# Bias row copies in 12 pieces behind the first attention's swaps, compression weights queued later, and idle products at the start

## The chip, the cores and the metric

One core of one Trainium2 chip runs the whole program once. The metric is the device time in microseconds of that core, as a median of several runs. TensorE (PE) multiplies matrices, VectorE (DVE), ScalarE (ACT) and GpSimd (POOL) do the elementwise work, and SyncE (SP) issues every data transfer of this kernel. A number such as L510 is a line of the kernel.

## The reference, cut to what matters

512 tokens of width 1024 go through a first block and then twice through a hybrid layer. All numbers are 32-bit floats.

```
# first block
h = rms_norm(x, pre_mix_g);  proj = h @ w_in          # q, k, v of two attentions, gates
oa = diff_attention(rope(qa), rope(ka), va)           # 4 heads of 128, causal
ob = softmax-weighted sum of three dilated windows over rope(qb), rope(kb), vb   # 3 groups x 4 heads
x = x + rms_norm((g_a * (oa @ w_a_out) + g_b * (ob @ w_b_out)) @ w_mix_out, post_mix_g)
u = causal_depthwise_conv(rms_norm(x, pre_ffn_g) @ w_up)
x = x + rms_norm((gelu(gate) * val) @ w_down, post_ffn_g)

# hybrid layer, twice
kc, vc = silu(blocks(k_cmp) @ cmp_w1) @ cmp_w2, ...   # the compression
logits = q @ k.T * scale + rel_bias[head, t5_bucket(distance)]   # windows of 512 and of 128
x = x + rms_norm((attentions * silu(z)) @ w_out, g_post)
```

The rotation `rope` pairs each row of a head with a partner row, so the kernel needs a copy of q and k with its rows swapped. The relative bias depends on the distance alone.

## The kernel before, in words

**Products.** Every large product keeps 32-bit precision by splitting both operands in a high and a low part: `mm3` issues three matmuls (L195 to L197) of 128 x 128 by 128 x 512. A weight tile of 512 KB is loaded into `wraw` (L169, three buffers), ScalarE rounds it to `whi` (L162), VectorE subtracts to `wlo` (L163), four buffers each. `fm` makes one tile of 128 output rows for all 512 tokens: 24 matmuls.

**Order.** The program is written stage by stage, and a planner orders each engine's instructions at compile time by a simulated timeline. So a load whose buffer is free can stand far ahead of its stage in the program. Within an engine, and on SP's queue, instructions then run strictly in that order; SP hands all its transfers to one hardware queue. `tc.issue_after(ins)` orders the instructions traced under it behind `ins` on the same engine.

**Start.** `ident` (L150), two halves of the first token tile (`load_x`, L357), the gain row `grow` (L366), first weights, more token tiles. Two products with a row of ones spread the gains (`g_pre`, L371). `pre_norm` makes each token tile's mean square, scales it (`xn`, L236), transposes it with `ident` on PE (`tp`, L224) and splits it to `hT`. The products `pv` for the values of the first attention follow.

**First attention** (L525 to L597). For each of four heads `a_project` makes q and k, each through `rope`: ScalarE copies the product to `rq` (L506), SP copies the swapped rows into `rs` (L510; four transfers here, two in the second attention), VectorE multiplies both with cosine and sine and adds (L512 to L521). `a_attend` of a head stands one head behind: scores (L544), subtract the maximum (L548), exponential, values. Products for the values of the second attention (`tm_cols(VB, ...)`) stand after head 0's projection.

**Bias and mask** (L599 to L602, written behind the first attention). `m_b` is the second attention's mask. `bias_tables` loads the buckets (`rb`, `hot`), makes the bias of each distance with three small products (`bv`, L398) and stores them to `vrow` in DRAM (L404). `bias_rows` writes each row 128 times to `spill` in DRAM (L409), in two DRAM to DRAM transfers of [4, 128, 640] and [8, 128, 384]. The hybrid layers read `spill` once, at L786, with a step that shifts each row.

**Second attention** (L607 to L687): `b_project` with six swaps for each head, `b_attend` with scores (L641, L645), the maximum (`nm`, L650), exponential and values.

**Later.** The gates and `w_mix_out`; the feed-forward loop over `w_up` (L748 to L757); `w_down` in `post_norm`; then the layers. There the compression reads its weights into four buffers `w1` of the tag `e4`, 16 transfers for each layer (L990); the first attention's outputs `oa` use the same tag before.

Of the kernel before, what the change touches and what calls it, by code (L numbers as in the profile page):

```python
# [9 lines left out]
F32 = mybir.dt.float32  # L10
# [84 lines left out]
def emit(tc, A, out):  # L95
    nc = tc.nc
# [13 lines left out]
    def c2(name, dt=F32):  # L110
        return bp.tile([128, 512], dt, name=name, tag="c2", bufs=16)
# [25 lines left out]
    def bank(tag, name):  # L137
        if tag == extra["tag"]:
            extra[tag] += 1
            if extra[tag] % 3 == 0:  # L140
                tag = "x"
        return pp.tile([128, 512], F32, name=name, tag=tag,
                       bufs={"pj": 2, "s": 2, "t": 2, "x": 1, "o": 1}[tag])
# [3 lines left out]


    ident = cp.tile([128, 128], F32, name="ident")
    nc.sync.dma_start(ident, A["c_ident"])  # L150
    mhalf = cp.tile([128, 4], F32, name="mhalf")
    nc.vector.memset(mhalf, -0.5)

# [2 lines left out]

    ahead = []
    evacuated = {}

    def split(src, hi, lo, engine=nc.vector):  # L160

# [3 lines left out]
    def wtile(src3):  # L165

        a, b = src3.shape[1], src3.shape[2]
        raw = wp.tile([128, a, b], F32, name="wraw", tag="wraw", bufs=3)
        nc.sync.dma_start(raw, src3)  # L169
        return raw  # L170

    def wsplit(raw):
# [95 lines left out]
    def gain(pool, name, src, off=0):  # L268
        g = pool.tile([128, D], F32, name=name, tag="gain", bufs=caps[pool].get("gain", 2))
        nc.sync.dma_start(g, bcast(src, D, off))  # L270
        return [g[:, u:u + 512] for u in (0, 512)]
# [77 lines left out]
    mp_stack, mp = phase("mp", r=4, pb=2, pt=4, qk=11, tb=5, P=2)  # L349
# [4 lines left out]
    def load_x(t):  # L354
        xt = [c2("xt") for _ in range(2)]
        for u in range(2):
            nc.sync.dma_start(xt[u], A["x"][0, t * 128:(t + 1) * 128, u * 512:u * 512 + 512])  # L357
        return xt

    def v_weights(c0, k0):  # L360
        return wtile(wrows(W1, PW, 0, k0, 2, c0, 512))


    xt = [load_x(0)]
    grow = mp.tile([1, D + 128], F32, name="grow", tag="P", bufs=caps[mp]["P"])
    nc.sync.dma_start(grow[:, 0:D], bass.AP(tensor=A["pre_mix_g"].tensor, offset=A["pre_mix_g"].offset,  # L366
                                    ap=[[D, 1], [1, D]]))
# [2 lines left out]
    for u in range(2):  # L370
        nc.tensor.matmul(g_pre[u], grow[:, D:], grow[:, u * 512:u * 512 + 512],  # L371
                         start=True, stop=True)
# [9 lines left out]
    spill = [dp.tile([4, 128, 640], F32, name="spill0"), dp.tile([8, 128, 384], F32, name="spill1")]  # L382
    vrow = [dp.tile([4, 640], F32, name="vrow0"), dp.tile([8, 384], F32, name="vrow1")]

    def bias_tables():
        rb = small("rb", 12, 1, mp)
        nc.vector.memset(rb, 1.0)
        rel = A["rel_bias_2"]
        nc.sync.dma_start(rb[0:32].rearrange("p (a b) -> p a b", b=1),
                          bass.AP(tensor=rel.tensor, offset=rel.offset,  # L390
                                  ap=[[1, 32], [32, 12], [1, 1]]))
        hot = [t2(mp, "pb", "hot") for _ in range(2)]
        wv = [os("wv") for _ in range(2)]
        for i in range(2):
            nc.sync.dma_start(hot[i][0:33], A["c_hot"][:, 512 * i:512 * i + 512])
        for i, c0, w, r0, m in ((0, 0, 512, 0, 4), (1, 0, 128, 0, 4), (1, 128, 384, 4, 8)):
            ps = bank("t", "bv")
            nc.tensor.matmul(ps[0:m, :w], rb[0:33, r0:r0 + m], hot[i][0:33, c0:c0 + w],  # L398
                             start=True, stop=True)
            nc.vector.tensor_copy(wv[i][0:m, c0:c0 + w], ps[0:m, :w])  # L400
        for dest, src in ((vrow[0][:, 0:512], wv[0][0:4]),
                          (vrow[0][:, 512:640], wv[1][0:4, 0:128]),
                          (vrow[1], wv[1][0:8, 128:512])):
            nc.sync.dma_start(dest, src)  # L404

    def bias_rows():

        for dest, src in zip(spill, vrow):
            nc.sync.dma_start(dest, src[:, None].to_broadcast(dest.shape))  # L409

    def hact(k):
        return hT[0][:, k], hT[1][:, k]
# [1 line left out]
    def tm_cols(c0, dest, dil=1):  # L414

        ws = {}
        for half in range(2):
            ps = [bank("pj", "pv") for _ in range(2)]  # L420
            for k0 in range(0, 8, 2):
                if not half:
                    ws[k0] = wsplit(c0 == VA and early.pop(k0, None) or v_weights(c0, k0))
                hi, lo = ws[k0]
                for e in range(2):
                    t = 2 * half + e
                    tok = slice(t * 128, (t + 1) * 128) if dil == 1 else slice(t, 512, 4)
                    for k in range(2):
                        mm3(ps[e], hT[0][:, k0 + k, tok], hT[1][:, k0 + k, tok],
                            hi[:, k], lo[:, k], k0 + k == 0, k0 + k == 7)  # L430
            for e in range(2):
                nc.scalar.copy(dest[2 * half + e], ps[e])
# [66 lines left out]
    nc.sync.dma_start(gdh, cols(A["diff_head_g"], 0, 1).rearrange("p a b -> p (a b)"))  # L499
    nc.vector.tensor_scalar(gdh, gdh, 1.0 - (0.8 - 0.6 * math.exp(-0.3 * 0)), None, op0=OP.mult)  # L500

    def rope(ps, cos, sin, sw, perm=None):


        q = t2(mp, "r", "rq")
        nc.scalar.copy(q, ps)  # L506
        s = t2(mp, "r", "rs")
        for b in range(0, 128, sw):
            o = b ^ sw
            nc.sync.dma_start(s[b:b + sw], q[o:o + sw])  # L510
        o = t2(mp, "qk", "qk")
        nc.vector.tensor_mul(q, q, cos)  # L512
        nc.vector.tensor_mul(s, s, sin)
        if perm is None:
            nc.vector.tensor_add(o, q, s)
        elif perm == "q":
            v = lambda a: a.rearrange("p (n i r) -> p n r i", n=4, r=4)
            nc.vector.tensor_add(o.rearrange("p (n r i) -> p n r i", n=4, r=4), v(q), v(s))
        else:
            v = lambda a: a.rearrange("p (j r) -> p r j", r=4)  # L520
            nc.vector.tensor_add(o.rearrange("p (r j) -> p r j", r=4), v(q), v(s))  # L521
        return o
# [64 lines left out]
        nc.scalar.activation(oa[h], pt, AF.Copy, scale=gdh)  # L587

    vb = [[c2("vb") for _ in range(4)] for _ in range(3)]
    prev = None  # L590
    for h in range(5):
        cur = a_project(h) if h < 4 else None
        if h == 0:
            tm_cols(VB, vb[0])
        if prev is not None:
            a_attend(h - 1, *prev)
        prev = cur  # L597

    m_b = mp.tile([128, 1536], F32, name="m_b")  # L599
    nc.sync.dma_start(m_b, A["c_masks"][:, :1536])  # L600
    bias_tables()
    bias_rows()  # L602

# [97 lines left out]
    for c in range(8):  # L703
        acc = c2("mixT")
        mixT.append(acc)
        for br in range(2):
            ps = fm(W1, PW, 0, GT + br * D + c * 128, hact, tag="s")
# [3 lines left out]
            src, W = oT[br], A[("w_a_out", "w_b_out")[br]]  # L711
            ps = fm(W, D, 0, c * 128, lambda k: (src[0][k], src[1][k]), kt=4, tag="t")
# [35 lines left out]
    for c in range(NF):  # L748
        ps = fm(A["w_up"], 2 * DFF, 0, c * 128, hact, tag=FT[2 * c % 5], parts=2 if c < 2 else 1)
        gt = conv(ps, c)  # L750
        ps = fm(A["w_up"], 2 * DFF, 0, DFF + c * 128, hact, tag=FT[(2 * c + 1) % 5],
                parts=2 if c < 2 else 1)
# [4 lines left out]
        yT.append(y)  # L757

    g_post = gain(fp, "g_post", A["post_ffn_g"])
    g_pre = gain(fp, "g_pre", A["norm_pre_2"])  # L760
    hT = new_hT()
    post_norm(A["w_down"], 0, NF, lambda k: yT[k], g_post, lambda t: xs[t], fp,
# [145 lines left out]
    def layer(l):  # L908
# [20 lines left out]
        ps = [bank("t", "ctp"), bank("t", "ctp"), bank("s", "ctp")]  # L929
        for t in range(4):  # L930
# [21 lines left out]
            s = slice(t * 128, t * 128 + 128)  # L952
# [8 lines left out]
        ps = fm(W2, PW2, l * D * PW2, A_KV, hact)  # L961
# [3 lines left out]
        o = A["cmp_pos_2"].offset + l * 4096  # L965
# [18 lines left out]
        for j0 in range(0, 16, 4):  # L984
            ws = []
            for e in range(2):
                w = e4("w1")
                ws.append(w)
                for u in range(2):
                    nc.sync.dma_start(  # L990
                        w[ROWS[u]].rearrange("p (j h) -> p j h", j=4),
                        bass.AP(tensor=w1.tensor,
                                offset=w1.offset + ((l * 2 + e) * 2048 + (u * 16 + j0) * 64) * 128,
                                ap=[[128, 64], [64 * 128, 4], [1, 128]]))
            for j in range(4):
                for e in range(2):
                    nc.tensor.matmul(hid[32 * e:32 * e + 32, 0:128], st[e][:, j0 + j],
                                     ws[e][:, j * 128:j * 128 + 128],
                                     start=(j0 + j == 0), stop=(j0 + j == 15))
# [17 lines left out]
        ps = bank("t", "kc")  # L1017
# [9 lines left out]
        ps = bank("t", "vc")  # L1027
# [3 lines left out]
        for h in range(4):  # L1031
            s = slice(32 * h, 32 * h + 32)
# [7 lines left out]
        raw = wp.tile([128, 2, 4, 128], F32, name="wraw", tag="wraw", bufs=3)  # L1040
        for k in range(2):
            o = uq.offset + (l * 256 + k * 128) * 384
# [206 lines left out]
```

## Time and profile before

| | us |
|---|---|
| median of 3 runs | 1475.95 |
| lowest and highest | 1475.46, 1477.06 |
| the profiled execution | 1476.09 |
| its span, first to last instruction | 1474.3 |
| PE busy | 1438.1 |
| DVE busy | 806.2 |
| ACT busy | 633.6 |

The span is the time from the first to the last instruction; the profiled execution's own time lies 1.8 us above it. PE is busy in nearly all of it. An engine's busy time says little here for the others; what matters is where PE has to wait, and at which granted clock it runs.

### The profile page before, as it was taken

The numbers are of one execution on the slowest core, as the hardware profiler recorded it, in microseconds if no ns is written. First come the engines' busy times: TensorE is split into PE (matmuls) and PEld (weight loads), VectorE is DVE, ScalarE is ACT, GpSimd is POOL, SyncE is SP. The second block draws the span as 40 slices with busy tenths as digits, with TensorE's granted clock in tenths as the row PEclk, the third lists the DMA queues.
The fourth block names the chain that finished last, engine by engine and source line by source line (L and its number), as shares of the span: only waits on it lengthen the run. The fifth ranks groups of instructions, "written<-read, shape, count | busy, mean of one in ns | idle before, by whom it ended". The sixth has DMA issues, their size and how long they took to land.

```text
span 1474.3 us, 19531 instructions
## 1 busy us (share of the span) xinstructions
PE 1438.1 (98%) x7362; PEld 1152.6 (78%) x7362; DVE 806.2 (55%) x1558; ACT 633.6 (43%) x1346; POOL 119.1 (8%) x188
## 2 busy tenths in 40 slices
PE   8999999599999999999999999999999989999998
PEld 6878877487888888888888888877777777767776
DVE  6454365465443535755555334566666366475745
ACT  5334343233422334533333323526666354475643
POOL 1000000000000014000000002610000064000000
PEclk9999999799999999999999999999999999999999
DMA  6642244644133526433333332633112224311111
GB/s 202 170 115 74 67 109 130 152 108 107 58 108 99 171 72 95 138 100 100 93 93 100 100 93 65 180 103 101 30 57 58 73 71 107 89 44 44 58 44 72
DMA packets 210356, 141.91 MB, mean 96 GB/s; under 512 B 37123, under 2 KB 189711, under 8 KB 210262
## 3 DMA queue, kind: packets, MB, share of 16 engines
q1 hardware_dynamic: 210262, 140.67, 34.4%
q8 instruction: 58, 0.95, 0.3%
q14 instruction: 36, 0.29, 0.1%
HBM read 129.08 MB, written 5.00 MB: 91 GB/s over the span
## 4 chain that ended last, share of the span: by engine, by line
PE 91%; POOL 2%; DMA 2%; DVE 2%; ACT 1%; SPq 1%; issue 1%; DVEq 0%; POOLq 0%; ACTq 0%
PE fm L196 16%; PE fm L197 16%; PE fm L195 16%; PE tm L195 6%; PE tm L197 6%; PE tm L196 6%; PE pt L815 3%; PE pv L196 2%; PE pv L195 2%; PE pv L197 2%; PE oA L820 2%; PE S L544 1%; PE S L902 1%; PE S L1114 1%; PE S L903 1%; PE oC L820 1%
## 5 line engine op out<-in xcount | busy, mean ns | idle before, releaser
L195 PE MATMUL fm<-hT,whi 128*128 128x512 f32 (+1 forms) x1056 | 408.7, 388 | 1.4 <-DVE hT L163 1.4
L196 PE MATMUL fm<-hT,whi 128*128 128x512 f32 (+1 forms) x1056 | 408.9, 387 | 0.0
L197 PE MATMUL fm<-hT,wlo 128*128 128x512 f32 (+1 forms) x1056 | 408.4, 387 | 0.0
L163 DVE TENSOR_TENSOR wlo<-wraw,whi 128x1024 fp32r<-128x1024 f32 (+1 forms) x209 | 245.7, 1177 | 242.6 <-ACT whi L162 237.1
L162 ACT CAST whi<-wraw 128x1024 fp32r<-128x1024 f32 (+2 forms) x218 | 219.4, 1008 | 324.4 <-PE fm L196 239.2
L196 PEld LDWEIGHTS fm<-hT,whi 128*128 128x128 f32 x1056 | 198.8, 188 | 42.5 <-issue 4.3
L195 PEld LDWEIGHTS fm<-hT,whi 128*128 128x128 f32 x1056 | 198.5, 188 | 41.4 <-DVE hT L163 1.6
L197 PEld LDWEIGHTS fm<-hT,wlo 128*128 128x128 f32 x1056 | 198.8, 188 | 40.9 <-issue 3.1
L196 PE MATMUL tm<-wlo,ah 128*128 128x512 f32 x368 | 143.9, 391 | 0.0
L197 PE MATMUL tm<-whi,al 128*128 128x512 f32 x368 | 142.9, 391 | 0.0
L195 PE MATMUL tm<-whi,ah 128*128 128x512 f32 x368 | 138.9, 392 | 0.0
L818 ACT COPY PT<-pt 128x512 f32<-128x512 f32 (+1 forms) x104 | 51.4, 520 | 85.2 <-PE pt L815 74.8
L195 PEld LDWEIGHTS tm<-whi,ah 128*128 128x128 f32 x368 | 69.1, 188 | 14.7 <-issue 0.7
L197 PEld LDWEIGHTS tm<-whi,al 128*128 128x128 f32 x368 | 69.1, 188 | 14.4 <-issue 0.3
L196 PEld LDWEIGHTS tm<-wlo,ah 128*128 128x128 f32 x368 | 69.1, 188 | 13.9
L259 POOL TENSOR_SCALAR post_v<-post_ss 128x1 f32<-128x1 f32 x16 | 9.3, 584 | 780.3 <-ACT y L255 659.5
L744 DVE SCALAR_TENSOR_TENSOR u<-fm,cw,u 128x511 f32<-128x511 f32 x88 | 65.4, 746 | 6.7 <-ACT u L741 5.3
L845 ACT ACTIVATE P<-P,nm 128x256 f32<-128x256 f32 (+3 forms) x96 | 53.6, 562 | 20.3 <-DVE nm L841 20.2
L815 PE MATMUL pt<-ident,P 128*128 128x128 f32 x352 | 56.5, 283 | 0.0
L815 PEld LDWEIGHTS pt<-ident,P 128*128 128x128 f32 x352 | 38.1, 141 | 19.3 <-issue 17.0
L196 PE MATMUL pv<-wlo,hT 128*128 128x512 f32 x128 | 52.2, 410 | 0.0
L197 PE MATMUL pv<-whi,hT 128*128 128x512 f32 x128 | 52.2, 409 | 0.0
(277 smaller groups left out, 1956.5 us busy)
## 6 DMA issues: line engine op xcount, KB each, us to landing
wraw<-in_w_in_dram SPq DMA_DIRECT2D x100, 512.0 KB, 4.1
wraw<-in_w_up_dram SPq DMA_DIRECT2D x44, 512.0 KB, 3.9
wraw<-in_w_down_dram SPq DMA_DIRECT2D x22, 512.0 KB, 3.6
wraw<-in_w_out_dram SPq DMA_DIRECT2D x16, 512.0 KB, 3.5
rs<-rq SPq DMA_DIRECT2D x48, 128.0 KB, 2.3
xt<-in_x_dram SPq DMA_DIRECT2D x16, 256.0 KB, 5.2
w<-in_cmp_w_dram SPq DMA_DIRECT2D x32, 128.0 KB, 3.0
wraw<-in_w_mix_out_dram SPq DMA_DIRECT2D x8, 512.0 KB, 3.8
```

The costliest lines, as they stand in the source:

```text
L162: a = nc.scalar.copy(hi, src)
L163: return a, engine.tensor_tensor(out=lo, in0=src, in1=f(hi), op=OP.subtract)
L195: nc.tensor.matmul(ps, ah, bh, start=first, stop=False)
L196: nc.tensor.matmul(ps, ah, bl, start=False, stop=False)
L197: nc.tensor.matmul(ps, al, bh, start=False, stop=last)
L544: nc.tensor.matmul(ps[:, :w], q[r, n * 128:(n + 1) * 128], k[r, :w], start=True, stop=True)
L744: nc.vector.scalar_tensor_tensor(u[:, d:], ps[:, :T - d], cw[:, j, c:c + 1], u[:, d:], op0=OP.mult, op1=OP.add)
L815: nc.tensor.transpose(pt[:, o + i * 128:o + i * 128 + 128], p, ident)
L818: nc.scalar.copy(at[:, :o], pt[:, :o])
L820: nc.tensor.matmul(O[ROWS[r], c0:c0 + w], v(r, kb), at[:, o:o + w], start=start, stop=stop)
L845: nc.scalar.activation(t[:, c:c + w], t[:, c:c + w], AF.Exp, bias=nm[:, u:u + 1], scale=-1.0, accum_out=den[:, u:u + 1])
L902: nc.tensor.matmul(ps[:, :w], q[:, s], kh[:, k0:k0 + w], start=True, stop=False)
```

## The change

Four edits:

- **Start.** The load of `ident` goes behind the first token tile's. A new `keep_busy(14)` clears a tile of 128 x 128 and lets PE multiply it 14 times with itself into a bank that nobody reads.
- **Bias and mask.** `m_b`'s load and `bias_tables` are traced after head 0's projection, and their transfers are ordered behind its last swap. `bias_rows` writes one row of one of the two tensors at a time; the 12 pieces go 4, 4 and 4 behind the last swaps of heads 1, 2 and 3.
- **Compression weights.** Their transfers are ordered behind the last weight load that was traced before `w_down`, which is the last of `w_up`.
- `wtile` and `rope` keep their last transfer's instruction for that.

```diff
     ident = cp.tile([128, 128], F32, name="ident")
-    nc.sync.dma_start(ident, A["c_ident"])
...
-        nc.sync.dma_start(raw, src3)
+        queued[:] = [nc.sync.dma_start(raw, src3).ins]
...
+    def keep_busy(n):
+        z = c2("z")[:, :128]
+        nc.vector.memset(z, 0.0)
+        ps = bank("o", "idle")
+        for _ in range(n):
+            nc.tensor.matmul(ps[:, :128], z, z, start=True, stop=True)
...
+    keep_busy(14)
     xt = [load_x(0)]
+    nc.sync.dma_start(ident, A["c_ident"])
...
-    def bias_rows():
-        for dest, src in zip(spill, vrow):
-            nc.sync.dma_start(dest, src[:, None].to_broadcast(dest.shape))
+    def bias_rows(i, rows):
+        d = spill[i][rows]
+        nc.sync.dma_start(d, vrow[i][rows][:, None].to_broadcast(d.shape))
...
-            nc.sync.dma_start(s[b:b + sw], q[o:o + sw])
+            swapped[:] = [nc.sync.dma_start(s[b:b + sw], q[o:o + sw]).ins]
...
+    m_b = mp.tile([128, 1536], F32, name="m_b")
     prev = None
     for h in range(5):
         cur = a_project(h) if h < 4 else None
         if h == 0:
+            with tc.issue_after(swapped[0]):
+                nc.sync.dma_start(m_b, A["c_masks"][:, :1536])
+                bias_tables()
             tm_cols(VB, vb[0])
+        elif h < 4:
+            i, rows = ((0, slice(0, 4)), (1, slice(0, 4)), (1, slice(4, 8)))[h - 1]
+            with tc.issue_after(swapped[0]):
+                for r in range(rows.start, rows.stop):
+                    bias_rows(i, slice(r, r + 1))
         if prev is not None:
             a_attend(h - 1, *prev)
         prev = cur
-    m_b = mp.tile([128, 1536], F32, name="m_b")
-    nc.sync.dma_start(m_b, A["c_masks"][:, :1536])
-    bias_tables()
-    bias_rows()
...
     g_post = gain(fp, "g_post", A["post_ffn_g"])
+    held = queued[0]
...
                 for u in range(2):
+                  with tc.issue_after(held):
                     nc.sync.dma_start(
                         w[ROWS[u]].rearrange("p (j h) -> p j h", j=4),
```

## Rows read from the trace of the kernel before

**Rows 1.** The page: busy us by engine; PE's granted clock in 40 slices, tenths.

```profile
PE 1438.1 (98%) x7362; PEld 1152.6 (78%) x7362; DVE 806.2 (55%) x1558; ACT 633.6 (43%) x1346; POOL 119.1 (8%) x188
...
PEclk9999999799999999999999999999999999999999
```

**Rows 2.** Waits of PE: line, releaser, us in total, times, longest us.

```profile
PE S L641 <- DVE nm L650: 15.9, 2, 15.0
PE g_pre L371 <- DMA grow<-in_pre_mix_g_dram: 5.1, 1, 5.1
```

**Rows 3.** Timeline, three engines: start us, us, instruction, count, [idle before <-releaser].

```profile
249.22 0.58 ACT L506 COPY rq<-fm 128x512 f32<-128x512 f32 x1
...
262.92 0.40 PE L195 MATMUL fm<-hT,whi 128*128 128x512 f32 x1
...
269.25 0.69 DVE L512 TENSOR_TENSOR rq<-rq,cosB 128x512 f32<-128x512 f32 x1 [18.68 <-DMA rs<-rq]
...
278.14 0.09 DVE L650 DVE_READ_ACCUMULATOR2_ANT nm<- 128x1 f32 x1
...
278.29 1.22 PE L641 MATMUL S<-qk 128*128 128x256 f32 x2 [14.96 <-DVE nm L650]
```

**Rows 4.** Timeline of SP's queue, 246 to 262 us.

```profile
241.67 5.42 SPq L409 DMA_DIRECT2D spill<-vrow  x1
247.14 14.26 SPq L990 DMA_DIRECT2D w<-in_cmp_w_dram  x4
261.44 0.94 SPq L510 DMA_DIRECT2D rs<-rq  x1
```

**Rows 5.** Windows: busy by engine, then granted clock, DMA share, GB/s.

```profile
249.00:257.00 8.00, 8.00 (x37) 6.64 (x36) 1.23 (x1) 1.84 (x3) 0.00 (x0) 1.00 0.51 194
257.00:260.00 3.00, 3.00 (x30) 2.45 (x29) 0.00 (x0) 0.00 (x0) 0.00 (x0) 1.00 0.37 126
...
263.30:278.30 15.00, 0.04 (x2) 0.02 (x1) 6.10 (x10) 1.80 (x3) 0.00 (x0) 0.62 0.90 202
278.30:284.50 6.20, 6.20 (x42) 3.53 (x42) 6.09 (x13) 1.64 (x7) 0.00 (x0) 0.55 0.51 131
```

**Rows 6.** The tile `rs`: its transfers' ns on SP (min/median/max), and landing.

```profile
L510 SPq DMA_DIRECT2D rs<-rq x80: 461/588/1664, 50.7 to 363.2; - x80
...
DMA to landing us min/median/max: 1.9/2.2/6.7
```

**Rows 7.** Waits of all engines, 48 to 186 us, the first attention.

```profile
DVE rq L512 <- DMA rs<-rq: 15.5, 5, 5.7
```

**Rows 8.** Timeline of PE at the bias products; DMA issues with us to landing.

```profile
231.53 1.02 PE L398 MATMUL bv<-hot,rb 33*4 33x512 f32 x2
...
m_b<-in_c_masks_dram SPq DMA_DIRECT2D x1, 768.0 KB, 7.1
```

**Rows 9.** Timeline of SP's queue between `w_up` and `w_down`.

```profile
767.67 0.37 SPq L169 DMA_DIRECT2D wraw<-in_w_up_dram  x1
773.12 0.34 SPq L169 DMA_DIRECT2D wraw<-in_w_down_dram  x1
```

**Rows 10.** Timeline of the start, SP's queue and PE.

```profile
0.72 0.39 SPq L150 DMA_DIRECT2D ident<-in_c_ident_dram  x1
...
5.05 3.75 PE L371 MATMUL g_pre<-grow 1*128 1x512 f32 x4 [5.05 <-DMA grow<-in_pre_mix_g_dram]
8.73 1.11 PE L224 MATMUL tp<-ident,xn 128*128 128x128 f32 x4
...
12.36 0.79 PE L195 MATMUL pv<-whi,hT 128*128 128x512 f32 x1
12.95 0.63 PE L196 MATMUL pv<-wlo,hT 128*128 128x512 f32 x1
...
14.69 0.40 PE L196 MATMUL pv<-wlo,hT 128*128 128x512 f32 x1
...
19.72 1.03 PE L224 MATMUL tp<-ident,xn 128*128 128x128 f32 x8
```

## What the change should do, worked out before it ran

> **What bounds the kernel now.** I read the busy shares first, then the list of what TensorE (PE) waited for, then the place of its one long wait in the timeline, and last the DMA side of that place. PE is busy for 1438.1 of 1474.3 us [rows 1], so only 36.2 us of the span are to be had from waiting, and what any other engine does counts only where it makes PE wait or lowers its clock. The slices of the granted clock have one dip, the ninth slice [rows 1]. The list of PE's waits [rows 2] has eight lines; two are of weight: 15.0 us in one piece at the scores of the second attention (L641, waiting for VectorE's `nm` of L650), and 5.1 us at the very start (L371, waiting for the first loads). None of the eight lines is in the first attention.
>
> The long wait, followed backwards [rows 3]: PE's last product starts at 262.92 and the next at 278.29, when VectorE (DVE) has done L650 at 278.14. DVE had stood from 250.57 to 269.25, 18.68 us, at the rope's product of L512 for the swapped copy `rs`. That copy's source, `rq`, was there at 249.22 + 0.58 = 249.80 from ScalarE (ACT). So the swap was wanted at 249.80 and came 19 us later. Why: it stands on SP's queue behind other DMAs [rows 4]. The second copy of the bias rows held SP for 5.42 us, the four loads of compression weights behind it for 14.26 us, and the swap was issued at 261.44. While SP stood, the DMA engines were not full [rows 5]: share 0.51 from 249 to 257, then 0.37. A share near a half is what eight busy engines of sixteen would give. The bias copies have outer sizes 4 and 8. I read this as two copies lying on 4 and 8 of the 16 engines, with the queue of those few engines full and SP unable to hand anything on.
>
> **The stall's worth.** PE's idle time is 14.96 us [rows 3]. Then the clock is down: 0.62 mean over the stall and 0.55 from 278.3 to 284.5 [rows 5], that is, nearly all at the lower level (1.2 GHz of 2.4). The work of these 6.2 us would take 6.2 x 0.55 = 3.4 us at the full clock, a loss of 2.8. Together 17.8 us. Behind it PE is dense again, so nothing gives the lost time back in the kernel before.
>
> If the swap goes out at 249.80, it lands some 2.2 us later, the median of 80 swaps [rows 6], at about 252.0 instead of 269.25. L650 follows as it does now, 278.14 - 269.25 = 8.9 us behind, at 260.9, and PE wants it at 263.3. There are 2.4 us to spare. **Term: -17.8 us.** What is late next there is the 0.9 us that the same line has left, which I leave standing.
>
> **The copies in 12 pieces.** 1280 KB and 1536 KB are written as before, now in four pieces of 320 KB and eight of 192 KB, each queued behind the last swap of heads 1, 2 and 3. Each piece has 128 rows of its own as its outer size. The rate of one engine follows from the stretch of 249 to 257: 194 GB/s / (0.51 x 16) = 23.8 GB/s; from 257 to 260, 21.3. Over 16 engines that is 380 GB/s, so the groups of 1.31, 0.79 and 0.79 MB take 3.4, 2.1 and 2.1 us. On SP four issues cost 4 x 0.59 = 2.4 us (an issue's median, [rows 6]). Queued behind SP's pieces are the next weight load and the next head's swaps. A swap that comes right behind the largest group is late by at most 2.4 + 3.4 = 5.8 us. The row to hold against that: in the first attention DVE waited five times for swaps, 15.5 us in all and up to 5.7 us at once [rows 7], and PE waited for nothing there. So the price lies between 0 and 3 x 5.8 = 17.4 us if every group met a swap with no cover. I take 0, since the row of 5.7 us is nearest, and keep up to 6 (one group met fully) in the range. If the cover is gone, each microsecond shows as a wait of PE at L544.
>
> First the row, then a rule: the shares of 0.51 and 0.37 fit copies that use few engines. The Trainium skill (DMA: Bandwidth & Descriptors, section "Why a DMA increments its semaphore by 16 and not by 1") says that a DMA takes the largest number of engines up to 16 that divides the slowest dimension larger than 1. By that rule the old copies had 4 and 8 engines, and a piece of [1, 128, n] has 16; this trace agrees with the first half and has no row for the second. If size-1 dimensions counted, the pieces would run on one engine, which is the rival that ends slower.
>
> **The bias tables and the mask, moved from the start to behind head 0's swap.** Three loads, three small products (`bv`) and three stores. The products only move (the largest takes 1.02 us, [rows 8]), so they cost nothing new. But before, the tables were loaded some 200 us ahead of the products; now PE may reach `bv` before they land. Bounds: 0, and 7.1 us, the landing of the mask that goes ahead of them on the queue [rows 8]. I take +0.5. Behind SP's wait for the `bv` results stand weight loads, which run several tiles ahead.
>
> **Compression weights of the first layer.** Eight loads leave 247 to 268 and go behind the last `w_up` load at 767.67. SP is idle from 768.0 to 773.1 [rows 9], 5.1 us; eight issues at 0.59 take 4.7. They are needed in the first layer, some 200 us later. Cost 0; without that gap it would be 4.7 us of SP time on loads that are themselves ahead of use. **Edits with one answer:** the second-layer loads are traced behind the same load, which is long past; cost 0.
>
> **The start.** `ident` goes behind the first input tiles, so these leave 0.39 us earlier [rows 10]; `grow` keeps its place. Fourteen products of zeros run on PE, which is idle until 5.05. Each of these f32 products is two records, as the two products of L371 are four [rows 10], so 28 records. Four transposes take 1.11 us at 8.73 and eight take 1.03 at 19.72 [rows 10], so PE starts at about half its rate. The 28 take 28 x 0.28 = 7.8 us at the first and 28 x 0.13 = 3.6 at the second rate. From about 1.1 us they would end between 4.7 and 8.9. The gain, if PE is at full rate sooner: the transposes lose 0.6, the first three weight products 3 x 0.23 (0.63 against 0.40), plus 0.39: -1.7. The loss, if they run to 8.9: the gain products of `grow` start 3.9 us late and take half of their 3.75, so +2.0. What hides a loss is that ScalarE's next splits wait for loads in any case. I take **-1.0**, bounds -2 to +2.
>
> **Sum.** 1476.09 (the profiled execution; its span is 1474.3, with 1.8 us around it) - 17.8 + 0 + 0.5 + 0 - 1.0 = 1457.8. The median of the three runs is 0.14 below the profiled execution, so 1457.6.
>
> **The rivals.**
> Partly given back: PE meets the moved work in the first attention, by one group in front of a swap (5.8) or by `bv` waiting out the mask's landing (7.1). For: an order planned at compile time need not know how long these loads take. Against: DVE waits of 5.7 us there cost PE nothing. Time: 1457.6 + 5.8 to 7.1, about 1464.
> The stall only moves: another filler takes the place of the copies on SP, or the second attention's DVE order is late for a reason of its own. For: only 2.4 us to spare were found. Against: the other 20 waits for swaps are about 2 us each, and PE does not see them. Time: 1457.6 + 17.8 = 1475.4, no change.
> Slower: the pieces run on one engine. 2.88 MB at 23.8 GB/s are 121 us; PE went on for 13.5 us after `rq` was ready (249.80 to 263.3), so each of the three groups would be covered for about that long, and 121 - 3 x 13.5 = 80 us are left: 1538. It decides from the point where a group lasts over 13.5 us, at 1.31 MB that is four engines or fewer. For: the outer size is 1. Against: the shares for outer sizes 4 and 8, and the 128 rows inside.
>
> **How the numbers follow.** Forecast as summed, 1454 to 1461: 0.62. Partly given back, 1461 to 1472: 0.22. More gained than priced, below 1454, by the small waits of the second attention and the start's full -2: 0.05. Stall only moved: 0.05. Slower: 0.06. A measurement tells about 0.2% (3 us) from no change. Faster 0.89, same 0.05, slower 0.06. The range runs from 1453 to 1467: 0.03 lies below, 0.17 above.
>
> **What would show it.** Right: no wait of PE at L641 over 1 us, no dip of the clock after the start, DVE's longest wait at L512 under 6 us, each group of pieces at a DMA share near 1 for 2 to 4 us, the compression loads near 770. Wrong: a new wait of PE at L544 or `bv` (partly given back), SP held for more than 5 us behind a piece (few engines), or a later start of the first `pv` product than 12.36.

## The result and the profile after

The changed kernel takes 1458.25 us (median of 4 runs, 1457.85 to 1459.91) against 1476.24 for the kernel before (4 runs): a ratio of 0.988, 95% interval 0.9863 to 0.9897, that is 18.0 us less. The prediction was 1457.6, with a range of 1453 to 1467. The profiled execution took 1459.91, the slowest of its four, with a span of 1458.1.

The page of the kernel after, busy us by engine and the granted clock in 40 slices, against [rows 1]:

```profile
PE 1440.6 (99%) x7390; PEld 1158.5 (79%) x7390; DVE 806.4 (55%) x1559; ACT 634.2 (43%) x1346; POOL 120.6 (8%) x188
...
PEclk9999999999999999999999999999999999999999
```

The dip of the clock in the ninth slice is gone. What PE waited for in the kernel after (line, releaser, us in total, times, longest), against [rows 2]:

```profile
PE tp L224 <- DVE xn L236: 5.3, 3, 3.0
...
PE S L659 <- DVE nm L668: 0.9, 1, 0.9
```

The wait of 15.0 us at the scores of the second attention is not there any more; the 0.9 us of the same line is. L659 and L668 are the lines 641 and 650 of before; L523 and L525 are the swap and the rope's first product (L510 and L512), L420 the copies (L409), L1010 the compression weights (L990).

SP's queue in the kernel after, around the first of the three groups of pieces, and the pieces' own line (ns on SP, min/median/max, then us to landing), against [rows 4] and [rows 6]:

```profile
86.30 2.41 SPq L523 DMA_DIRECT2D rs<-rq  x4
88.75 2.51 SPq L420 DMA_DIRECT2D spill<-vrow  x4
91.36 0.54 SPq L169 DMA_DIRECT2D wraw<-in_w_in_dram  x1
92.50 2.73 SPq L523 DMA_DIRECT2D rs<-rq  x4
...
L420 SPq DMA_DIRECT2D spill<-vrow x12: 589/596/596, 88.8 to 119.9; - x12
...
DMA to landing us min/median/max: 3.8/4.3/5.0
...
91.30:96.00 4.70, 4.70 (x22) 3.67 (x20) 2.71 (x7) 2.21 (x6) 0.00 (x0) 1.00 0.84 274
```

Four pieces hold SP for 2.51 us, and after one weight load the swaps of the next head's q follow, 1.2 us later. The last line is a window (after the busy times: granted clock, DMA share, GB/s): the group and the loads around it keep the DMA engines at a share of 0.84. VectorE waits 6.24 us for that swap, as the timeline of its L525 shows, but the list of PE's waits has none in the first attention:

```profile
90.29 0.69 DVE L525 TENSOR_TENSOR rq<-rq,cosA 128x512 f32<-128x512 f32 x1 [2.02 <-DMA rs<-rq]
100.25 0.69 DVE L525 TENSOR_TENSOR rq<-rq,cosA 128x512 f32<-128x512 f32 x1 [6.24 <-DMA rs<-rq]
```

### The profile page after: what moved, and what is told of

Its sections match the earlier page's. It is cut to its first block, busy times and chain, and to the rows that moved or that the text cites. A ratio compares the mean times of both kernels' runs of the same rounds, so it can differ in the third digit from the quotient of the medians.

```text
span 1458.1 us, 19594 instructions
## 1 busy us (share of the span) xinstructions
PE 1440.6 (99%) x7390; PEld 1158.5 (79%) x7390; DVE 806.4 (55%) x1559; ACT 634.2 (43%) x1346; POOL 120.6 (8%) x188
## 4 chain that ended last, share of the span: by engine, by line
PE 94%; POOL 2%; DVE 2%; DMA 1%; ACT 1%; issue 1%; SPq 0%; DVEq 0%; POOLq 0%; ACTq 0%
PE fm L196 17%; PE fm L195 17%; PE fm L197 17%; PE tm L195 6%; PE tm L197 6%; PE tm L196 6%; PE pt L834 3%; PE pv L195 2%; PE pv L197 2%; PE pv L196 2%; PE oA L839 2%; PE S L557 1%; PE S L921 1%; PE S L1134 1%; PE S L922 1%; PE oC L839 1%
## 5 line engine op out<-in xcount | busy, mean ns | idle before, releaser
L834 PEld LDWEIGHTS pt<-ident,P 128*128 128x128 f32 x352 | 38.1, 141 | 19.3 <-issue 17.0
L195 PE MATMUL pv<-whi,hT 128*128 128x512 f32 x128 | 53.1, 418 | 0.0
L197 PE MATMUL pv<-whi,hT 128*128 128x512 f32 x128 | 52.6, 412 | 0.0
```

The lines of the kernel that those rows point to most:

```text
L195: nc.tensor.matmul(ps, ah, bh, start=first, stop=False)
L197: nc.tensor.matmul(ps, al, bh, start=False, stop=last)
L834: nc.tensor.transpose(pt[:, o + i * 128:o + i * 128 + 128], p, ident)
```

## The experiments

The theory behind the prediction: the two whole copies lie on few DMA engines, fill their queue and hold SP, so the swap behind them is late. The rivals: the plain amount of data in front of the swap, however spread; the compression weights as fillers on SP; the mere place of the copies. For the start: the chain through `grow` and `xn` against the clock.

| kernel | us, median (runs) | ratio to before, 95% interval |
|---|---|---|
| before, weights queued later | 1472.84 (10) | 0.9976, 0.9967 to 0.9986 |
| before, copies turned | 1468.11 (4) | 0.9944, 0.9929 to 0.9959 |
| before, copies in 12 pieces | 1464.57 (4) | 0.9926, 0.9911 to 0.9941 |
| before, turned and weights later | 1463.02 (4) | 0.9915, 0.9900 to 0.9930 |
| before, pieces and weights later | 1463.18 (4) | 0.9908, 0.9891 to 0.9926 |
| before, the start's edits alone | 1475.95 (11) | 1.0001, 0.9992 to 1.0010 |
| changed, copies whole | 1467.94 (4) | 0.9948, 0.9933 to 0.9963 |
| changed, weights not queued later | 1458.29 (4) | 0.9883, 0.9867 to 0.9900 |
| changed, no idle products | 1458.92 (4) | 0.9884, 0.9869 to 0.9899 |
| changed, 7 idle products | 1458.80 (4) | 0.9884, 0.9868 to 0.9901 |
| changed, 28 idle products | 1463.19 (4) | 0.9915, 0.9901 to 0.9929 |

### Copies turned, in the old place

```diff
-            nc.sync.dma_start(dest, src[:, None].to_broadcast(dest.shape))
+            nc.sync.dma_start(dest.rearrange("h p n -> p h n"),
+                              src[:, None].to_broadcast(dest.shape).rearrange("h p n -> p h n"))
```

> The kernel before with one edit: the two copies of the bias rows have their dimensions turned, so that 128 is the outer one (before 4 and 8). Same place, same two transfers, same 2.88 MB, and every other instruction stands in the same order. Theory of few engines: 2.88 MB over 16 engines at 23.8 GB/s each take 7.6 us from 240.8, SP is held under 2 us by each copy, the swap is issued before 253 instead of 261.4, and PE's wait at L641 falls from 15.0 to at most 3 us, with no dip of the clock: 1458.5 to 1462 us. Rival of bytes (2.88 MB and 1 MB of compression weights stand ahead of the swap, however spread): nothing changes, 1476. Rival of the fillers (the compression weights hold SP): nothing changes either, 1476.

SP's queue in this run, a window while the copies are in flight, VectorE's and PE's wait, and the copies' landing:

```profile
242.43 1.31 SPq L409 DMA_DIRECT2D spill<-vrow  x2
243.79 9.75 SPq L990 DMA_DIRECT2D w<-in_cmp_w_dram  x4
253.58 1.57 SPq L510 DMA_DIRECT2D rs<-rq  x2
...
244.50:257.50 13.00, 13.00 (x59) 10.78 (x58) 3.47 (x4) 4.08 (x5) 0.00 (x0) 1.00 0.97 281
...
261.20 0.69 DVE L512 TENSOR_TENSOR rq<-rq,cosB 128x512 f32<-128x512 f32 x1 [9.00 <-DMA rs<-rq]
...
PE S L641 <- DVE nm L650: 6.8, 2, 5.9
...
DMA to landing us min/median/max: 11.8/13.2/14.7
```

On every engine and on SP's queue all instructions stand in the same order as before, so the 8.2 us gained come from the spread of the copies alone. The share is 0.97 where it was 0.51 in [rows 5], the two copies hold SP for 1.31 us where the second of them alone held it for 5.42, and PE waits 5.9 us instead of 15.0. So few engines were the cause of more than half of PE's wait, and of 8.2 of the 18.0 us. But the expected 1458.5 to 1462 was missed. While the copies are in flight the 16 engines give 281 GB/s at a share of 0.97, some 18 GB/s each, for the copies and the loads behind them together, not the 23.8 each of the prediction; the copies land 11.8 to 14.7 us after their issue and not within 7.6; and SP is again held, for 9.75 us, at the first loads behind them. The amount of data in front of the swap is a cause of its own.

### Compression weights queued later, alone

```diff
+    held = queued[0]; g_pre = gain(fp, "g_pre", A["norm_pre_2"])
...
+                  with tc.issue_after(held): nc.sync.dma_start(
```

> The kernel before with the compression weights alone queued behind the last w_up load; the two copies stay whole and in place. Theory of few engines: the first four engines hold 0.52 MB each, 22 us at 23.8 GB/s, so they are busy from 241.7 to about 263; the swap goes out near 250 but its rows on these engines land near 264 instead of 269. PE's wait at L641 is 7 to 11 us: 1467 to 1471 us. Rival of the fillers: the wait is gone, 1458 to 1461. Rival that the compression weights don't matter: 1476.

SP's queue and the waits of VectorE and PE:

```profile
242.25 5.86 SPq L409 DMA_DIRECT2D spill<-vrow  x2
248.16 12.32 SPq L510 DMA_DIRECT2D rs<-rq  x2
...
DVE rq L512 <- DMA rs<-rq: 16.3, 2, 15.9
...
PE S L641 <- DVE nm L650: 12.9, 2, 12.0
```

With the loads gone, the swap itself is what SP cannot hand on, for 12.32 us. So the loads did not hold SP of themselves; they stood behind the copies, as the swap does now. PE's wait falls by 3.0 us and the time by 3.5; both miss what I expected (7 to 11 us of wait, 1467 to 1471). The planner also orders the second attention's work otherwise in this run than before (from 270 to 304 us), so the 3.5 us are not those of the loads alone.

### Turned, and weights later

The two edits above together.

> The kernel before with the turned copies (128 outer) and with the compression weights queued later, all else in place; against the run with the turned copies alone it takes 0.5 MB of loads out from between copies and swap. Theory of what lies in front: the copies end near 257 as with the turned copies alone, the swap right behind them lands near 258 instead of 260.3, PE's wait at L641 is 3 to 4 us instead of 5.9: 1463 to 1466 us. Rival of the fillers (the loads cost SP and the queue more than their bytes): no wait is left, 1458 to 1460.

```profile
241.51 1.31 SPq L409 DMA_DIRECT2D spill<-vrow  x2
...
250.52 4.21 SPq L510 DMA_DIRECT2D rs<-rq  x2
...
258.01 0.69 DVE L512 TENSOR_TENSOR rq<-rq,cosB 128x512 f32<-128x512 f32 x1 [6.74 <-DMA rs<-rq]
...
PE S L641 <- DVE nm L650: 3.7, 2, 2.9
```

The swap lands near 258 and PE waits 2.9 us; the time is at the lower end of what was expected. PE, VectorE and ScalarE have the same order here as in the run before this one, and the turning is worth 9 to 10 us (9.0 by the ratios to before, 9.8 by the medians). In front of the late swap now stand the copies' 2.88 MB, another swap and one weight load of 512 KB; that it is the copies that still make it late is argued from their size and not tested by itself. That the fillers were the main cause is refuted by the first two runs; in the old place they were worth 3 to 5 us (3.5 with whole copies, 5.1 with turned ones), the planner's other order included.

### Twelve pieces in the old place, without and with the weights later

```diff
-            nc.sync.dma_start(dest, src[:, None].to_broadcast(dest.shape))
+            for r in range(dest.shape[0]):
+                d = dest[r:r + 1]
+                nc.sync.dma_start(d, src[r:r + 1][:, None].to_broadcast(d.shape))
```

> The kernel before with the two copies cut into the same 12 pieces as in the changed kernel, but left in their old place. Theory of what lies in front (the swap waits for the 2.88 MB ahead of it; spread and rate only set how long): if the pieces go at the 300 GB/s of the changed kernel's groups, they end 10 us after 242, the swap lands 1 to 3 us after it is wanted, PE waits 0 to 3 us at L641: 1459 to 1463 us. If they go at the 200 GB/s of the turned copies, they end near 257 and PE waits 3 to 6 us: 1465 to 1468. Rival of place (only moving the copies helps): 1472 or more.

> The kernel before with the copies as 12 pieces in their old place and the compression weights queued later: the whole change but for the place of the copies and the start. Theory of what lies in front (the old place puts swaps right behind 2.88 MB, whatever the pieces): PE still waits 1 to 4 us at L641, 1460 to 1463 us, so 2 to 4 us of the gain belong to the place. Rival (pieces and later weights are enough): 1458 to 1459.5, no wait over 1 us.

First the pieces alone (SP's queue, a window, waits of PE), then with the weights later:

```profile
241.95 9.18 SPq L411 DMA_DIRECT2D spill<-vrow  x12
251.33 2.98 SPq L512 DMA_DIRECT2D rs<-rq  x4
...
249.00:257.00 8.00, 8.00 (x37) 6.64 (x36) 1.64 (x2) 2.59 (x3) 0.00 (x0) 1.00 0.99 292
...
PE S L643 <- DVE nm L652: 2.7, 3, 1.4
```

```profile
241.38 10.08 SPq L409 DMA_DIRECT2D spill<-vrow  x12
251.56 2.47 SPq L510 DMA_DIRECT2D rs<-rq  x4
...
PE S L641 <- DVE nm L650: 2.8, 3, 1.0
```

In the old place twelve issues hold SP for 9 to 10 us, and swaps stand right behind them. PE's waits are small, yet 11.0 us are gained where 18 were to be had, between the two ranges that were expected. With the weights later 12.7 us are gained, just outside the expected 1460 to 1463, and the four runs spread from 1458.62 to 1464.65. The planner puts the second attention in another order in both runs than before, so they do not say what the cut alone is worth. With pieces and later weights in the old place the median is 4.9 us above the changed kernel. That speaks for the place, but the orders of the two differ, and the lowest of the four runs is level with the changed kernel.

### The changed kernel with whole copies

```diff
-                for r in range(rows.start, rows.stop):
-                    bias_rows(i, slice(r, r + 1))
+                if h < 3:
+                    bias_rows(i, slice(0, (4, 8)[i]))
```

> The changed kernel with the two copies whole (outer sizes 4 and 8), one behind head 1's last swap and one behind head 2's. Theory of few engines: each copy lies on 4 and 8 engines for 13 and 8 us at 23.8 GB/s, SP is held behind the first, head 2's swap lands 7 to 10 us late, VectorE waits over 8 us at L525 and PE waits 3 to 10 us in the first attention: 1461 to 1469 us. Rival of place (behind a swap nothing is urgent, so the cut into pieces is worth nothing): 1458.3, no wait of PE over 1 us.

SP's queue, VectorE, the windows that follow, and PE's wait:

```profile
86.98 0.71 SPq L420 DMA_DIRECT2D spill<-vrow  x1
87.79 4.60 SPq L169 DMA_DIRECT2D wraw<-in_w_in_dram  x1
92.50 3.38 SPq L523 DMA_DIRECT2D rs<-rq  x4
...
104.77 0.69 DVE L525 TENSOR_TENSOR rq<-rq,cosA 128x512 f32<-128x512 f32 x1 [12.54 <-DMA rs<-rq]
...
88.00:92.00 4.00, 4.00 (x20) 2.80 (x19) 3.50 (x8) 2.63 (x6) 0.00 (x0) 1.00 0.23 82
100.00:104.00 4.00, 1.98 (x9) 1.31 (x7) 0.00 (x0) 0.00 (x0) 0.00 (x0) 1.00 0.26 95
106.60:115.30 8.70, 8.70 (x14) 4.29 (x15) 6.39 (x12) 4.82 (x11) 0.00 (x0) 0.50 0.33 107
...
PE S L557 <- DVE nm L561: 4.6, 1, 4.6
```

The place alone is not enough: 9.7 us are lost against the pieces, with the same order on PE, VectorE, ScalarE and GpSimd, and within what was expected. While the copy of outer size 4 is in flight the share is 0.23 from 88 to 92, about four engines of sixteen, and 0.26 again from 100 to 104. VectorE waits 12.54 us for the swap behind it, PE waits 4.6 us, and when PE starts again at 106.6 its granted clock is 0.50 for 8.7 us, which loses half of them, 4.4 us. Together 9.0 of the 9.7 us.

### The changed kernel without the later weights

```diff
-                  with tc.issue_after(held):
+                  if True:
```

> The changed kernel without the later queueing of the compression weights: eight loads come back among the second attention's swaps, three of them ahead of one swap and five ahead of the next; PE's and VectorE's orders are unchanged. Theory of what lies in front: 0.4 to 0.6 MB and 2 to 3 us of SP ahead of a swap that has 2.4 us to spare, so PE waits 0 to 1.5 us: 1458.3 to 1460 us. Rival of the fillers: VectorE waits over 5 us for these swaps and PE 3 us or more: 1461 or more.

The eight loads come back at 233 to 241 us, three of them ahead of one swap and five ahead of the next; the other engines' orders are the same as in the changed kernel. VectorE's waits for swaps from 230 to 290 us:

```profile
DVE rq L525 <- DMA rs<-rq: 10.5, 4, 3.5
```

The longest is 3.5 us, PE waits no more there than in the changed kernel (0.9 us), and the median is 1458.29, the same as with the loads queued later. Once the copies are elsewhere, the queueing of the weights is worth nothing that these runs can tell.

### The start

```diff
-    keep_busy(14)
+    keep_busy(7)        # or 28, or the line left out
```

> The kernel before with the start's edits alone (14 idle products, ident's load written behind the first token tile). The prediction's term was -1.0 us. Against it: executions with one and the same start reach the full matmul rate anywhere between 13.5 and 17.1 us, so that the start's worth is lost in it: 1475.9 with or without, within 0.7 us.

> The changed kernel without its 14 idle products. Theory A (the idle products end at 6.9 us, after grow has landed, and so put the first xn of VectorE behind the first weight split): the g_pre products start near 5, the first xn near 7.3 instead of 9.9, the first pv near 12.4 instead of 14.0, and the time falls by 1.0 to 2.0 us, to about 1456.7. Theory B (the later start comes from the mask's and the bias tables' leaving the start): pv still near 14.0 and the same time. Theory C (idle products pay by the warm clock): 0.5 to 1.5 us slower.

> The changed kernel with 7 idle products instead of 14. They take about 1.07 to 4.0 us and end before grow lands at about 5. Theory A: the g_pre products start near 5 and the first xn near 6.5 to 7.3, pv near 12.4; time as without idle products or up to 0.7 us less, 1456.0 to 1456.9. Theory B: as with 14, 1458.2. Theory C: between the time with 14 and the time without.

> The changed kernel with 28 idle products instead of 14. They end near 10 us instead of 6.9, so the g_pre products, xn and the first pv come 1 to 2 us later than with 14 (pv near 15 to 16), but PE has no idle gap before them, the granted clock is 1.00 from then on and no pv product takes 0.63 us. Theory A (the chain through grow decides): 1 to 2 us slower, 1459.5 to 1460.5. Theory C (the clock decides): equal or up to 1 us faster, 1457.3 to 1458.5.

The start in the kernel after (SP, PE and VectorE; in the window lines the third number from the end is the granted clock), against [rows 10]:

```profile
0.72 0.40 SPq L375 DMA_DIRECT2D ident<-in_c_ident_dram  x1
1.07 5.79 PE L367 MATMUL idle<-z 128*128 128x128 f32 x28 [1.07 <-DVE z L364]
6.79 1.98 PE L382 MATMUL g_pre<-grow 1*128 1x512 f32 x4
8.74 1.23 DVE L163 TENSOR_TENSOR wlo<-wraw,whi 128x1024 fp32r<-128x1024 f32 x1 [7.58 <-ACT whi L162]
9.88 2.72 DVE L236 SCALAR_TENSOR_TENSOR xn<-xt,pre_r,g_pre 128x512 f32<-128x512 f32 x4
10.68 3.67 PE L224 MATMUL tp<-ident,xn 128*128 128x128 f32 x16 [1.91 <-DVE xn L236]
14.01 0.78 PE L195 MATMUL pv<-whi,hT 128*128 128x512 f32 x1
...
8.80:9.60 0.80, 0.00 (x0) 0.00 (x0) 0.80 (x1) 0.80 (x3) 0.00 (x0) 0.96 0.80 218
9.60:10.60 1.00, 0.00 (x0) 0.00 (x0) 1.00 (x3) 0.35 (x2) 0.47 (x2) 0.50 0.94 334
```

The idle products do warm PE: the four `g_pre` records take 1.98 us instead of 3.75. But VectorE now stands at the first weight split ahead of `xn`, PE has nothing from 8.8 to 10.7, the granted clock goes to 0.50 at about 9.6, and the first `pv` comes at 14.01 instead of 12.36, at half rate. With 7 products it comes at 9.59, without any at 11.17:

```profile
9.59 0.80 PE L195 MATMUL pv<-whi,hT 128*128 128x512 f32 x1 [0.81 <-ACT hT L162]
```

```profile
11.17 0.78 PE L195 MATMUL pv<-whi,hT 128*128 128x512 f32 x1
```

So theory A had the order of events right, and its times wrong: the first `pv` does come earlier, but the three kernels with 14, 7 and no idle products are within 0.7 us of each other, with single runs that overlap. Nor does theory C, the warm clock, show in their times. With 28 products the loss is plain, 4.9 us, more than the 1 to 2 expected: `grow`'s products start at 10.44, the first `pv` at 16.50, and the last copy of the first attention's values starts at 43.0 instead of 39.8. Of the loss, 2.8 us stand in the two traces by 54 us; where the rest comes from was not found. The clock falls in that run all the same: 1.00 at 13.3 to 13.8, 0.50 from 14.2, after PE had been busy to 12.4 and idle for 0.9 us. The start's edits alone change nothing that can be measured (ratio 1.0001).

Why nothing shows: by the end of this stage the difference is smaller than that between executions. In six of them (before and its five variants with the old start, without the start's edits) the first instructions of all engines stand in the same order, and the last copy of the first attention's values starts between 38.4 and 40.0 us, mean 39.3. In four with 14 idle products whose first instructions of PE, VectorE and ScalarE stand in one common order (three of the changed kernel's forms and the start alone) it starts between 38.1 and 39.9, mean 39.2.

## Why the prediction was right, step by step

**The stall's worth, -17.8.** Right, and for the reason given. The stall and its dip are gone and the runs are 18.0 us apart. Counted product by product in the two timelines, PE in the changed kernel is 1.7 us behind that of before at 258 us and 16.1 us ahead of it at 321, so 17.8 us are gained in this stretch, and nothing to speak of is gained or lost after it. The two profiled executions are only 16.2 apart in span, since the one of before had the earliest start of its kind (38.4) and the one of after a late one (39.8): 1.4 us that lie within what executions differ by.

**Where the stall comes from.** The mechanism was right but not the whole of it. Few engines: shown, by the turned copies in the old place (PE's wait from 15.0 to 5.9, orders unchanged) and by the whole copies in the new place (9.7 us lost, share 0.23). The Trainium skill's rule (DMA: Bandwidth & Descriptors, section "Why a DMA increments its semaphore by 16 and not by 1"), that the slowest dimension above 1 sets the number of engines, agrees with both: 0.23 for outer size 4, and 0.97 for 128 rows. What the prediction lacked is that 2.88 MB on all engines still make a swap behind them late, so that PE waits 5.9 us with the weights between copies and swap and 2.9 without. Five kernels with the weights queued later put sizes to it. By their ratios to before, whole copies in the old place gain 3.5 us, spread copies there 12.5 (turned) or 13.6 (pieces), whole copies in the new place 7.7, and the changed kernel 17.7 to 18.0. So the spread is worth 9 to 10 us in either place, and the place 4 to 5.5 us with either kind of copy. Between the places the planner's orders differ too, so the second figure is less sure than the first. The later weights add 3 to 5 us in the old place and nothing in the new one.

**The pieces' cost, 0.** Right in the sum: SP is held 2.51 us for each group (2.4 expected), and the next swap is late, VectorE waiting 6.24 us (at most 5.8 expected), with no wait of PE. The mis-sized term is the rate. The prediction took 23.8 GB/s per engine times 16 = 380 GB/s; the first group's window shows 274 GB/s at a share of 0.84, some 20 GB/s per engine, and the turned copies 281 at 0.97. That PE would not wait was taken from the nearest row and not worked out, and it was near: with whole copies a wait of 12.54 us cost PE 4.6, so by an estimate from these two numbers about 8 us of such a wait are covered there, and the pieces used 6.24 of them. There is some luck in this term.

**Bias tables, +0.5.** They cost nothing in sight: no wait of PE at the small products, although they now run at 63 and 70 us, soon after their loads.

**Compression weights, 0.** Right, as the run without their queueing shows. They went out at 752.11 in 5.35 us (4.7 expected, near 770), between two weight loads:

```profile
752.11 5.35 SPq L1010 DMA_DIRECT2D w<-in_cmp_w_dram  x8
```

**The start, -1.0.** Its steps were wrong. The time did not move measurably, with an interval of -1.2 to +1.5 us by the ratio of the run with the start's edits alone; -1.0 is still inside that interval, so it is the traces and not the time that speak against the term. Three steps of it failed. `ident` did not move: the planner still issues it first, so the 0.39 us were never there. The warm clock did not last to the products that were to gain by it. And the idle products changed the planner's order on VectorE, which put `xn` behind the weight split. The error stayed small because the term was small, and half of it was cancelled by the +0.5 of the bias tables, which did not come either.

**The rivals.** The stall did not move, and the pieces do not run on one engine: three groups hold SP for 2.5 us each. The rival of the price given back in the first attention came about only with whole copies.

**The signs named beforehand.** Three did not come out as written, though the time did: VectorE's longest wait for a swap is 6.24 us and not under 6, the first group's window has a share of 0.84 over 4.7 us and not near 1 for 2 to 4, and the first `pv` starts at 14.01, later than 12.36, which was named as a sign of being wrong. It was one for the start's term alone.

## What to carry to other kernels

A swap or any short transfer that a strict queue of work waits for can be made late by all that was queued before it. Here a bulk copy did least harm right behind the last urgent transfer of a group, in portions whose delay of the next one was covered, and not where its buffers happened to be free. Look at the DMA share while a transfer runs: here 0.23 and 0.5 with a blocked queue went with copies of outer size 4 and 8, and making 128 the outer size gave 8 to 10 us with nothing else moved. Idle products ahead of the first real work are worth measuring alone, with more and fewer of them, before anything is booked for them.

## What was not expected of the hardware

Executions with one and the same start differ there by more than the edit was to bring: in six, of before and five variants with the same order of first instructions, the first weight product at full rate (0.40 us and not 0.63) starts anywhere from 14.46 to 17.12 us.

With the copies from DRAM to DRAM on all engines, the rate per busy engine is lower than with the copies on a few: 281 GB/s at a share of 0.97 (18 GB/s each) for the turned copies, and 292 at 0.99 (18 each) for the 12 pieces in the same place, against 194 at 0.51 (23.8 each). The first two windows hold other loads too, and no run here tells whether these or the copies are the slower part.

The granted clock fell to 0.50 at 14.2 us in the run with 28 idle products, with PE busy until 12.4 and idle for less than 1 us before the transposes:

```profile
10.00:12.40 2.40, 2.40 (x9) 0.98 (x7) 0.97 (x1) 2.04 (x4) 0.45 (x1) 1.00 1.04 387
12.40:13.30 0.90, 0.02 (x1) 0.00 (x0) 0.90 (x3) 0.50 (x3) 0.48 (x2) 1.00 1.07 405
...
14.20:14.60 0.40, 0.40 (x3) 0.40 (x4) 0.40 (x2) 0.40 (x2) 0.00 (x0) 0.50 0.97 328
```

Why it fell can't be read from these rows and stays open.
